# The residual kept in DRAM during two gated networks, block products in the first of them from the seventh pair on, and modulation dots spread over three stages

## The chip, the cores and the metric

The kernel runs on one core of a Trainium2 chip. The number compared is the device time of one execution in microseconds. The engines of the core that matter here are TensorE (PE, with its weight loads on a row of their own, PEld), VectorE (DVE), ScalarE (ACT), GpSimd (POOL) and SyncE (SP). All of them run their instructions in the order in which the program gives them. DMAs are issued from SP, and those that add to what lies at their target are issued from POOL.

## The reference, cut to what matters

One step of a small diffusion backbone on 128 context tokens and 512 latent tokens, width 1024. Two layers: a state-space mixer, a gated convolutional network, a differential attention, and a second gated network. Everything is float32 in and out. In every layer a modulation vector of six parts (shift, scale and gate of both halves) comes from the conditioning:

```python
def modulation(cvec, w, b):
    m = jax.nn.silu(cvec) @ w + b
    return jnp.split(m[:, None, :], 6, axis=-1)

def conv_ffn(h, up_w, conv_w, conv_b, down_w):
    u = dwconv(h @ up_w, conv_w, conv_b)
    a, v = jnp.split(u, 2, axis=-1)
    return (jax.nn.silu(a) * v) @ down_w
...
        xp = xp + p_g1 * op
        xs = xs + s_g1 * os_
        ffn_p = (ffn_up_w[i], ffn_conv_w[i], ffn_conv_b[i], ffn_down_w[i])
        xp = xp + p_g2 * conv_ffn(modulate(xp, norm_ffn_g[i], p_sh2, p_sc2), *ffn_p)
        xs = xs + s_g2 * conv_ffn(modulate(xs, norm_ffn_g[i], s_sh2, s_sc2), *ffn_p)
```

The hidden width of the networks is 2816, that is 22 tiles of 128 rows for `a` and 22 for `v`.

## The kernel before, in words

**Layout.** Activations stand transposed: 8 tiles of 128 features by 640 tokens. Every float32 product is made of three products of rounded operands: each operand is split into a high part (a rounded copy, made by ACT) and a low part (the rest, made by DVE, or by a scaled ACT copy and an accumulating DMA). A weight block of 128x128 against 640 tokens so takes three passes, each in two matmuls of 256 and 384 columns (`HALF`), that is six matmuls.

**Weights.** `weight_units` lists all weight tiles in the order of use. `prefetch` loads them into four raw buffers with DMAs on SP, `cast` makes high and low parts, one or two tiles (`deep`) ahead of their use. For the units in `summed` the low part is made by ACT (a copy times -1) and a DMA from POOL that adds the weight from DRAM; for the others by a DVE subtraction (L107, `wlo`).

**A gated network (`ffn`).** It works in pairs: one tile of `a` and one of `v` (`up`), then the convolution, SiLU and product (`epilogue`, tiles `ca`, `cv`), then a split of the result (`mh`, `ml`). After some pairs (`SUB`) their rows go through the down projection (`project_out`, tile `po`, 8 output tiles), and `gate_add` adds the gated result to the residual `x` on DVE, reading PSUM. The last stretch of the down projection is `project_last`, which also starts the next norm. An ordinary pair is 2 tiles x 8 k-blocks x 6 = 96 matmuls of 320 columns on average. In the second network, pairs 4 to 21 take a seven-product scheme over the whole width (`pair8`, `NS` 4): sums of weight blocks (tiles `s`, made on DVE) and sums of activation blocks (tiles `T`, made once by `operands`), 7 blocks x 4 x 3 = 84 matmuls of 320 columns. In the first network, only pairs 16 to 21 use such a scheme, over half of the width (`pair7`, `NS` 2): 30 k-blocks x 3 = 90 matmuls.

**The dots.** The modulation of the second layer is not a matmul: `mod_rest` loads 48 row tiles `mw` of `modT` (512 KB each) and takes two dot products of each with SiLU of the conditioning (`cbc`), by one DVE instruction of 1024 columns per dot (L620, 96 in all). It is a task that runs between matmuls: `hook` counts ticks, one per k-block (every second block in the product schemes), and a task goes on when its tick has come. All 96 dots lie in the first network.

**Buffers.** The pool `acts` has 19 slots of 640 columns with the tag `f`: 8 of them hold the residual during the networks and the attention, 11 are left for the rest.

**Attention.** For every one of 8 heads: `q`, `k`, `v` tiles, then four blocks of scores (`sl`); the maximum is taken on DVE (`sm`), the exponential on ACT (`e`), the difference of two softmaxes on DVE (`w`), transposes and value products on PE (`wt`, `ov`), and a norm (`rs_v`, `rs_y`, `rs_a`, a small DMA `rsd` and back as `rbc`). `hold` adds a wait to an instruction without data between them; so far it ties scores and value products to earlier instructions. The framework orders each engine's stream from the program and priorities.

## Time and profile before

| | |
|---|---|
| median of three runs | 1849.85 us (1848.75 to 1850.08) |
| profiled execution, own time | 1847.95 us |
| its span | 1846.2 us, mean granted TensorE clock 0.994 |
| PE, PEld busy | 1802.7 us (98%), 1704.8 us (92%) |
| DVE, ACT, POOL busy | 1490.5 us (81%), 1038.7 us (56%), 49.2 us (3%) |
| DMA | 230.28 MB, mean 125 GB/s |
| first network, from its first projection to its last product | 567 to 1026 us |
| attention, heads | 1050 to 1325 us |
| second network | 1391 to 1827 us |

A row of stretches gives, for a window of the span, the busy time and the number of instructions of PE, PEld, DVE, ACT and POOL, then the granted clock, the mean busy share of the 16 DMA engines and their GB/s. PE is counted busy while any matmul is in flight, so that 98% says that there is nearly always one, not that each runs at the full rate; the rate is read from the chain of work, where a piece with its count of matmuls has its length. In the list of groups, the number behind the bar is the busy time, then the mean of one instruction.

### The profile page before, as it was taken

What the parts mean: (1) busy time and instruction counts of PE and PEld (TensorE: products, weight loads), DVE (VectorE), ACT (ScalarE), POOL (GpSimd) and SP (SyncE); (2) the same over time, 40 slices, a digit from 0 to 9 for tenths busy, and PEclk for the clock granted to TensorE, in tenths of its full rate; (3) what the DMA queues carried; (4) which work ended last, traced back from release to release, by engine and by line L of the source; (5) the groups of instructions that cost most, each with busy time, mean ns of one, the idle gap of its engine ahead of it and who ended that gap; (6) DMA issues with size and microseconds to landing.
All of it is one profiled execution on the core that took longest, in us unless ns stands there. A gap on an engine that the chain in (4) does not pass through costs nothing.

```text
span 1846.2 us, 33204 instructions
## 1 busy us (share of the span) xinstructions
PE 1802.7 (98%) x13070; PEld 1704.8 (92%) x13070; DVE 1490.5 (81%) x2969; ACT 1038.7 (56%) x1987; POOL 49.2 (3%) x60
## 2 busy tenths in 40 slices
PE   7999999999999999999999999999999999999997
PEld 5899999999989999999999988888899999999996
DVE  5689999999748999987585878777878877768784
ACT  3489686879326441343353556656636554746561
POOL 0000000000000000000000000000000010101110
PEclk9999999999999999999999999999999999999998
DMA  9844343445533556542122211211124445546451
GB/s 337 264 135 138 99 148 105 121 137 179 187 133 104 194 183 214 194 133 78 57 82 91 80 48 60 65 55 38 55 83 110 104 114 141 126 129 154 122 137 58
DMA packets 90051, 230.28 MB, mean 125 GB/s; under 512 B 10428, under 2 KB 17192, under 8 KB 89768
## 3 DMA queue, kind: packets, MB, share of 16 engines
q1 hardware_dynamic: 81256, 207.13, 34.8%
q0 software_dynamic: 8064, 20.52, 6.6%
q8 instruction: 102, 1.67, 0.4%
q10 hardware_dynamic: 576, 0.52, 0.1%
q14 instruction: 53, 0.43, 0.1%
HBM read 215.29 MB, written 5.96 MB: 120 GB/s over the span
## 4 chain that ended last, share of the span: by engine, by line
PE 86%; DVE 6%; ACT 3%; DMA 3%; issue 2%; SPq 0%; POOL 0%; DVEq 0%; POOLq 0%; ACTq 0%
PE up L110 27%; PE po L110 25%; PE z L110 6%; PE x L110 5%; PE st L110 5%; PE yp L110 3%; PE bc L110 3%; PE q L110 2%; PE k L110 1%; PE modrow L110 1%; PE sl L110 1%; ACT whi L101 1%; PE ov L110 1%; PE v L110 1%; ACT e L101 1%
## 5 line engine op out<-in xcount | busy, mean ns | idle before, releaser
L101 ACT ACTIVATE whi<-raw 128x1024 fp32r<-128x1024 f32 (+3 forms) x243 | 227.8, 939 | 277.3 <-PE po L110 167.4
L107 DVE TENSOR_TENSOR wlo<-raw,whi 128x1024 fp32r<-128x1024 f32 (+3 forms) x207 | 227.0, 1097 | 43.0 <-ACT whi L101 37.5
L104 DVE SCALAR_TENSOR_TENSOR xr<-po,mod,xr 128x256 f32<-128x256 f32 (+2 forms) x279 | 107.8, 432 | 108.9 <-PE po L110 108.8
L110 PE MATMUL po<-mh,whi 128*128 128x256 f32 (+1 forms) x704 | 166.9, 310 | 0.0
L110 PE MATMUL po<-ml,whi 128*128 128x256 f32 (+1 forms) x704 | 166.6, 309 | 0.0
L110 PE MATMUL po<-mh,wlo 128*128 128x256 f32 (+1 forms) x704 | 166.3, 309 | 0.0
L110 PE MATMUL up<-h01l,whi 128*128 128x256 f32 (+1 forms) x596 | 146.2, 308 | 0.0
L110 PE MATMUL up<-h01h,whi 128*128 128x256 f32 (+1 forms) x596 | 146.1, 310 | 0.1
L110 PE MATMUL up<-h01h,wlo 128*128 128x256 f32 (+1 forms) x596 | 145.6, 308 | 0.0
L110 PEld LDWEIGHTS po<-mh,whi 128*128 128x128 f32 x704 | 128.0, 188 | 0.7 <-ACT mh L101 0.5
L110 PEld LDWEIGHTS po<-ml,whi 128*128 128x128 f32 x704 | 128.2, 188 | 0.2 <-DVE ml L107 0.2
L110 PEld LDWEIGHTS po<-mh,wlo 128*128 128x128 f32 x704 | 128.2, 188 | 0.0
L110 PEld LDWEIGHTS up<-h01h,whi 128*128 128x128 f32 x596 | 108.9, 188 | 1.5 <-ACT uraw L101 1.1
L110 PEld LDWEIGHTS up<-h01l,whi 128*128 128x128 f32 x596 | 109.1, 188 | 0.0
L110 PEld LDWEIGHTS up<-h01h,wlo 128*128 128x128 f32 x596 | 109.0, 188 | 0.0
L110 PE MATMUL up<-h11h,whi 128*128 128x320 f32 (+1 forms) x368 | 107.3, 309 | 0.0
L110 PE MATMUL up<-h11l,whi 128*128 128x320 f32 (+1 forms) x368 | 107.2, 309 | 0.0
L110 PE MATMUL up<-h11h,wlo 128*128 128x320 f32 (+1 forms) x368 | 107.1, 309 | 0.0
L104 DVE SCALAR_TENSOR_TENSOR cv<-uraw,fcw,cv 128x511 f32<-128x511 f32 (+1 forms) x176 | 85.3, 545 | 14.8 <-ACT cv L101 14.8
L104 DVE SCALAR_TENSOR_TENSOR ca<-uraw,fcw,ca 128x127 f32<-128x127 f32 (+1 forms) x176 | 86.7, 545 | 8.8 <-ACT ca L101 7.5
L101 ACT ACTIVATE mh<-cv 128x640 fp32r<-128x640 f32 x44 | 32.5, 738 | 88.8 <-DVE cv L107 88.8
L101 ACT ACTIVATE whi<-s 128x512 fp32r<-128x512 f32 (+1 forms) x96 | 52.8, 571 | 52.2 <-DVE s L107 22.7
(531 smaller groups left out, 5074.4 us busy)
## 6 DMA issues: line engine op xcount, KB each, us to landing
raw<-in_w_up SPq DMA_DIRECT2D x88, 512.0 KB, 3.4
mw<-in_modT SPq DMA_DIRECT2D x48, 512.0 KB, 3.8
raw<-in_w_in SPq DMA_DIRECT2D x40, 512.0 KB, 5.5
rb<-rowd SPq DMA_DIRECT2D x40, 512.0 KB, 5.4
raw<-in_w_qkv SPq DMA_DIRECT2D x24, 512.0 KB, 3.3
mr<-in_mod SPq DMA_DIRECT2D x44, 256.0 KB, 5.2
wlo<-in_w_up POOLq DMA_DIRECT2D x17, 512.0 KB, 5.2
mp<-in_modp SPq DMA_DIRECT2D x32, 256.0 KB, 5.4
```

Of the source, the lines that this page charges most:

```text
L101: return self.nc.scalar.activation(out, in_, func, **k)
L104: return self.nc.vector.scalar_tensor_tensor(out, in0, s, in1, op0, op1)
L107: return self.nc.vector.tensor_tensor(out, a, b, op)
L110: return self.nc.tensor.matmul(out, lhsT, rhs, start=start, stop=stop, skip_group_check=more)
```

## The change

Six things are done together.

1. The first network uses `pair8` (`NS` 4) from its seventh pair on (`S0` 6), `pair7` is gone, and both networks project down after 4, 8, 12 and 16 pairs. The units of both networks get their low parts by ACT and DMA (`summed`).
2. In both networks, the residual is not in SBUF while the pairs run. `save` stores its 8 tiles to DRAM (`xd`) before; each of the first four down projections writes its gated result with ACT (`y`), and a DMA from POOL adds `y` to `xd`; `restore` loads the 8 tiles ahead of `project_last`. Attention saves and restores it too.
3. The memory so freed holds the activation sums (`sums`) and, from the first network to the end of attention, the dots' rows (pool `mod`). The `f` slots go from 19 to 11.
4. The dots run in three stages (`DOTS` 3, 34, 48): rows 0 to 2 at the end of the mixer, 3 to 33 in the first network, 34 to 47 in attention. SiLU of the conditioning is computed in the mixer and stored.
5. Each dot gets a wait (`hold`) on the last matmul that stood in the program before it; the number of ticks between dots is set by stage (`gap`, `rest`).
6. The pools follow each other with waits by tile (`reuse_waits`), and attention opens its pool after its first tiles.

```diff
-SUB = ((0, 8), (8, 15), (15, 22)), ((0, 4), (4, 8), (8, 12), (12, 16), (16, 22))
-MIDS = 9, 6
+SUB = (0, 4), (4, 8), (8, 12), (12, 16), (16, 22)
+MIDS = 6
-NS = 2, 4
-S0 = 16, 4
+NS = 4
+S0 = 6, 4
+DOTS = 3, 34, 48
-NF = 19
+NF = 11
...
+    def save(self, i):
+        if not self.xd:
+            self.xd = [self.dram.tile([P, T], F32, tag=f"xd{j}", name=f"xd{j}") for j in range(KT)]
+        self.nc.sync.dma_start(self.xd[i], self.x[i])
+
+    def restore(self):
+        self.open_x()
+        self.x = [self.xslot(f"xr{i}") for i in range(KT)]
+        for i in range(KT):
+            self.nc.sync.dma_start(self.x[i], self.xd[i])
...
-    def project_out(self, h, ks, g, tiles=range(KT)):
+    def project_out(self, h, ks, g, tiles=range(KT), to=None):
...
+            y = to(i)
             for hf in "AB":
-                self.gate_add(i, ps, g, hf)
+                for a, b, c in COND[hf]:
+                    self.act(y[:, a:b], self.cols(ps, hf, a, b), AF.Copy, scale=g[:, i, c:c + 1])
+            self.nc.gpsimd.dma_start(self.xd[i], y, accum_op=ALU.add)
...
-    def mod_rest(self, l, t0, pool):
+    def mod_rest(self, l, t0, t1, cb, alloc, junk_):
...
-                nc.vector.tensor_tensor_reduce(w if c else junk, w, cb[:, c, :], 1.0, 0.0, ALU.mult, ALU.add,
-                                               self.mod[l][:, t, c:c + 1])
-                yield 2 if self.down else 7
+                i = nc.vector.tensor_tensor_reduce(w if c else junk, w, cb[c], 1.0, 0.0, ALU.mult, ALU.add,
+                                                   self.mod[l][:, t, c:c + 1])
+                self.hold(i, [self.last])
+                yield self.gap + c * self.rest
...
         self.start_tiles(h)
         done = 0
-        self.deep = 2 if l else 1
+        self.deep = 2
...
+        self.xctx.close()
+        if not l:
+            self.open_mod()
...
+                    if not l and done == 3:
+                        junk = lambda: self.slot("sq", "junk", BF16, cols=1024, bufs=1)
+                        self.modtask = self.add(self.mod_rest(1, *DOTS[:2], self.cb, self.mod_row, junk), 1)
+                    self.gap, self.rest = 3 if done < S0[0] else 10, 0
...
+                    self.gap = 5 if s else 4
...
+        self.restore()
+        self.project_last(mid, range(*SUB[-1]), self.gate(l, 1), nextnorm, parts="CD" if l else "AB", save=not l)
...
+        self.gap, self.rest = 4, 3
+        early = self.add(self.mod_rest(1, 0, DOTS[0], self.cond_rows(row), row, junk), 8)
+        self.project_last(hy, range(8), self.gate(0, 0), nextnorm, save=True, before=[early])
...
+        self.gap, self.rest = 6, 0
+        dots = self.add(self.mod_rest(1, *DOTS[1:], self.cb, self.mod_row, junk), 10)
```

Line numbers move: what is L104, L107, L110, L620 before is L106, L109, L112, L674 in the changed kernel.

Three places of the order, before and after. First PE in the first network, in the pairs after the eighth (`h01h` and `h01l` are the high and low parts of the activations, `Th` and `Tl` those of their sums). Before, one k-block of an ordinary pair:

```order
L110 MATMUL up<-h01h_6528,whi_9048 128x256
L110 MATMUL up<-h01h_6528,whi_9048 128x384
L110 MATMUL up<-h01l_6529,whi_9048 128x256
L110 MATMUL up<-h01l_6529,whi_9048 128x384
L110 MATMUL up<-h01h_6528,wlo_9049 128x256
L110 MATMUL up<-h01h_6528,wlo_9049 128x384
```

The same engine in a pair of the changed kernel:

```order
L112 MATMUL up<-h01h_6581,whi_8933 128x320
L112 MATMUL up<-h01l_6582,whi_8933 128x320
L112 MATMUL up<-h01h_6581,wlo_8934 128x320
L112 MATMUL up<-Th_7105,whi_8984 128x320
L112 MATMUL up<-Tl_7106,whi_8984 128x320
L112 MATMUL up<-Th_7105,wlo_8985 128x320
```

Blocks of half the tokens against plain and summed operands stand where the six matmuls of a k-block stood: 84 in a pair instead of 96.

Second, DVE in the first network's first down projection before (`xr<-po` is the gated addition to the residual):

```order
L104 SCALAR_TENSOR_TENSOR xr_5172<-po,mod_112,xr_5172 128x128
L107 TENSOR_TENSOR wlo_8298<-raw_8159,whi_8297 128x1024
L620 ISA mw,mod_113<-mw,cbc 128x1024
L620 ISA mod_113 128x1
L620 ISA junk,mod_113<-mw,cbc 128x1024
L620 ISA mod_113 128x1
L620 ISA mw,mod_113<-mw,cbc 128x1024
L620 ISA mod_113 128x1
L104 SCALAR_TENSOR_TENSOR xr_5174<-po,mod_112,xr_5174 128x256 x2
```

In the changed kernel the additions stand on POOL, in the second down projection of the first network, as DMAs from `y` to `xd` between those that make low parts:

```order
L724 DMA ml_8473<-cv 128x640
L357 DMA xd_6145<-y 128x640
L724 DMA ml_8576<-cv 128x640
L357 DMA xd_6146<-y 128x640
L357 DMA xd_6147<-y 128x640
L357 DMA xd_6148<-y 128x640
L357 DMA xd_6149<-y 128x640
L357 DMA xd_6150<-y 128x640
L204 DMA wlo_8954<-in_w_up 128x1024
L357 DMA xd_6151<-y 128x640
L357 DMA xd_6152<-y 128x640
```

The gated addition has left DVE; ACT makes `y`, and eight accumulating DMAs per down projection are new in POOL's queue.

Third, DVE in attention, between the maxima (`sm<-sl`) of the third and the fourth block of a head, before:

```order
L107 TENSOR_TENSOR kl_13327<-k,kh_13326 128x640
L107 TENSOR_TENSOR rs_a<-rs_a,rs_y 128x160
L1305 RECIPROCAL sm<-sm 128x2
L104 SCALAR_TENSOR_TENSOR rs_a<-rs_a 128x160
L107 TENSOR_TENSOR sm<-sm,nlam 128x1
L104 SCALAR_TENSOR_TENSOR rs_y<-rs_a,rs_y 128x160
L104 SCALAR_TENSOR_TENSOR wp<-e_13391,sm,e_13394 128x128
L1297 TENSOR_REDUCE sm<-sl 128x1 x2
L107 TENSOR_TENSOR wlo_13599<-raw_13331,whi_13598 128x1024
```

The same place in a head of the changed kernel:

```order
L109 TENSOR_TENSOR kl_13872<-k,kh_13871 128x640
L109 TENSOR_TENSOR rs_a<-rs_a,rs_y 128x160
L674 ISA mw,mod_116<-mw,cb 128x1024
L674 ISA mod_116 128x1
L106 SCALAR_TENSOR_TENSOR rs_a<-rs_a 128x160
L1317 RECIPROCAL sm<-sm 128x2
L1309 TENSOR_REDUCE sm<-sl 128x1 x2
L106 SCALAR_TENSOR_TENSOR rs_y<-rs_a,rs_y 128x160
L109 TENSOR_TENSOR sm<-sm,nlam 128x1
L109 TENSOR_TENSOR wlo_14150<-raw_13876,whi_14149 128x1024
L1317 RECIPROCAL sm<-sm 128x2
L674 ISA junk,mod_116<-mw,cb 128x1024
```

A dot (`ISA mw,mod<-mw,cb`) stands ahead of the fourth maximum and another behind it; the last steps of the norm and `wp` have moved behind that maximum.

256 lines of the change are left out of this document (123 added, 133 removed).

## The prediction

> **What bounds the kernel now.** First the busy times of the page, then the chain of work that ended last, because only the chain tells the rate of the matmuls (start, length, piece with its count).
>
> ```profile
> PE 1802.7 (98%) x13070; PEld 1704.8 (92%) x13070; DVE 1490.5 (81%) x2969; ACT 1038.7 (56%) x1987; POOL 49.2 (3%) x60
> ```
>
> ```profile
> 582.75 105.61 PE up L110 x720
> 688.36 56.30 PE po L110 x384
> 744.66 98.63 PE up L110 x672
> 843.30 49.80 PE po L110 x336
> 893.10 42.34 PE up L110 x284
> ...
> 962.30 11.64 PE up L110 x78
> 973.94 40.50 PE po L110 x281
> ...
> 1569.40 49.26 PE up L110 x336
> 1618.66 28.16 PE po L110 x192
> ```
>
> Both networks are one unbroken row of matmuls at 147 ns each (105.61/720, 49.26/336). So in them time is the count of matmuls, as long as nobody else is late. Three points of reference: seven ordinary pairs took 98.63 us, 14.09 each; the last six, with the scheme over half of the width, took from 893.10 to 973.94, 80.84 us; four pairs of the second network in the scheme over the whole width took 49.26, 12.32 each. The second network thus already shows the speed that the first is to have.
>
> What the other engines do beside it, by stretches (PE, PEld, DVE, ACT, POOL busy; clock, DMA share, GB/s):
>
> ```profile
> 502.00:562.00 60.00, 60.00 (x466) 53.82 (x466) 29.56 (x65) 19.21 (x32) 0.00 (x0) 1.00 0.41 138
> 582.00:688.00 106.00, 106.00 (x724) 106.00 (x723) 105.59 (x179) 54.52 (x68) 0.00 (x0) 1.00 0.55 182
> 1050.00:1081.00 31.00, 27.71 (x202) 24.94 (x200) 27.05 (x51) 18.62 (x41) 0.00 (x0) 1.00 0.26 85
> 1155.00:1192.00 37.00, 35.48 (x250) 30.81 (x248) 28.74 (x58) 22.63 (x48) 0.00 (x0) 1.00 0.18 58
> 1408.00:1464.00 56.00, 54.21 (x354) 53.95 (x353) 45.16 (x87) 41.49 (x68) 8.00 (x9) 0.97 0.53 108
> 1619.00:1647.00 28.00, 28.00 (x193) 28.00 (x192) 20.42 (x44) 11.16 (x17) 1.75 (x2) 1.00 0.51 144
> 1647.00:1696.00 49.00, 49.00 (x336) 49.00 (x335) 37.54 (x71) 34.13 (x60) 7.88 (x9) 1.00 0.57 127
> ```
>
> The first network has DVE busy for 105.59 of 106 us without a gap on PE. A head of the attention (1155 to 1192) is a different thing: PE is held up for 1.5 us of 37, DVE busy for 28.74.
>
> **The change part by part.** Durations are of the profiled execution, which took 1847.95 us, 1.9 below the median of 1849.85; the sum is made against 1847.95 and 1.9 is added at the end.
>
> *Fewer matmuls.* Pairs 6 to 15 of the first network go from 96 to 84 matmuls, pairs 16 to 21 from 90 to 84: 10x12 + 6x6 = 156 fewer. In time: ten pairs at 14.09 and 80.84 make 221.7 us; sixteen at 12.32 make 197.0. That is -24.7 us, all on the path. The down projections keep their matmuls; five rounds instead of three change nothing in their rate (56.30/384 and 28.16/192 are both 147 ns).
>
> *The gated addition goes from DVE to ACT and a DMA.*
>
> ```profile
> L104 DVE SCALAR_TENSOR_TENSOR xr<-po,mod,xr 128x256 f32<-128x256 f32 (+2 forms) x279 | 107.8, 432 | 108.9 <-PE po L110 108.8
> L101 ACT ACTIVATE uraw<-up 128x320 f32<-128x320 f32 (+2 forms) x111 | 53.9, 491 | 9.4 <-PE up L110 9.1
> L620 DVE CUSTOM_DVE_ANT_0 mw<-mw,cbc 128x1024 f32<-128x1024 f32 x48 | 58.6, 1221 | 0.8
> ```
>
> Three instructions per output tile leave DVE, 1.30 us, and three of ACT from PSUM come, at most 0.49 each by the nearest row (`uraw`). A down projection has eight tiles: ACT gets 11.8 us more in 28 where it has 11.16, DVE 10.4 less. The cover is ACT's idle time, and PSUM, where three tiles stand in turn, each 3.5 us long: 0. Were ACT late, the PSUM banks would come free late and PE would stand.
>
> *The accumulating DMAs.* 64 new ones from POOL, 0.328 MB each. The nearest rows are those of the low parts, which POOL also issues (share of the 16 engines in the stretch):
>
> ```profile
> q0 software_dynamic: 1251, 3.01, 37.4%
> q1 hardware_dynamic: 1296, 3.15, 19.4%
> ...
> wlo<-in_w_up POOLq DMA_DIRECT2D x4, 256.0 KB, 5.9
> ```
>
> In 1647 to 1696, 3.01 MB took 37.4% of 49 us, 18.3 us of all 16 engines: 6.1 us per MB against 3.0 for plain loads (19.4% of 49 us for 3.15 MB). So one `y` costs 2.0 us. A round of four pairs and a down projection lasts 77 us; the engines are busy in it for 0.57x49 + 0.51x28 = 42 us now; eight `y` make 16, and in the first network some twelve dots of the round six rows of 0.524 MB, 9 us. That is 67 of 77 us: room, but loads and low parts queue behind each other in the down projections (14 + 16 + 5 us in 28) and finish later, while a low part has 5.9 us of its own and is used within a pair of 12.3. I take +2 us. The low end is 0; the high end is that an addition into DRAM takes twice as long as one into SBUF, 32 us per round, 83 of 77, four rounds: +24.
>
> The Trainium skill (DMA: Bandwidth & Descriptors, Anatomy of one DMA — SWDGE (gpsimd) path) fits a DMA issued from GpSimd as 2.0 us plus its bytes over 436 GB/s, which would make 0.75 us of moving for a `y`, a term of 0 and a sum 2 us lower; the low parts' 6.1 us per MB above differ from it by more than twice, so the row decides.
>
> *The dots in the first network.* 62 of 96 remain, 75.6 us of DVE at 1.22. The second network's rows are the base (37.54 of 49 in pairs, 20.42 of 28 in down projections): with 7 us of dots in four pairs, 44.5 of 49; with 8 us of dots and without the additions, 18 of 28. The tightest place is pairs 3 and 4, with about ten dots in 28 us, just after the activation sums (1408 to 1464 shows these with DVE at 45.16 of 56 and PE at 54.21). What would be late there is the low part of the next weight. I take +1 us; ends 0 and +6. The SP queue gets the rows (`mw`) past the weight loads as now.
>
> *The dots in attention.* 28 dots, 34.2 us, new to a stage where DVE and PE lean on each other. DVE over one head, with its idle times and what ended them:
>
> ```profile
> 1203.04 0.69 DVE L107 TENSOR_TENSOR wTl<-wt,wTh 128x512 fp32r<-128x512 f32 x1 [1.16 <-ACT wTh L101]
> ...
> 1215.08 0.29 DVE L107 TENSOR_TENSOR vl<-cv,vh 128x128 fp32r<-128x128 f32 x1 [1.16 <-ACT vh L101]
> 1217.15 1.56 DVE L1297 TENSOR_REDUCE sm<-sl 128x1 f32<-128x640 f32 x2 [1.78 <-PE sl L110]
> ...
> 1227.56 1.55 DVE L1297 TENSOR_REDUCE sm<-sl 128x1 f32<-128x640 f32 x2
> 1230.28 1.23 DVE L107 TENSOR_TENSOR wlo<-raw,whi 128x1024 fp32r<-128x1024 f32 x1 [1.17 <-ACT whi L101]
> ```
>
> Four dots fall on a head, 4.9 us, where 37 - 28.74 = 8.3 us are idle. By the order, one stands between the first and second maximum, one ahead of the third (1.16 and 1.78 us idle there), one ahead of the fourth, and one behind it (1.17 idle). Only the one ahead of the fourth stands where DVE has no idle time, from 1217.15 to 1227.56; there 1.2 us come and about 0.7 move behind the maximum: +0.5 us a head, 3.5 for seven heads, and a dot's 1.2 in the first head (27.05 of 31 busy). I take +5 us. Ends: 0, and half of the 34.2, +17.
>
> *The mixer's end.* Six dots and SiLU, some 11 us of DVE, ahead of the drain before the last three tiles. From 502 to 562 DVE is busy for 29.56 of 60: 0; without that cover 3.
>
> *Save and restore.* Eight loads of 320 KB, three times. Their memory comes free with the last block against `T`, two blocks (24 matmuls, 3.5 us) ahead of the end of the last pair; the first addition comes 36 matmuls, 5.3 us, after that. The like load of before landed in 4.6 us:
>
> ```profile
> xr<-in_xT SPq DMA_DIRECT2D x8, 320.0 KB, 4.6
> ```
>
> So 0; if SP stands on them, the next weights are late: +3 at the worst.
>
> Sum: -24.7 + 2 + 1 + 5 = -16.7; 1847.95 - 16.7 + 1.9 = 1833 us.
>
> **The rivals.**
>
> *All of it hidden.* Second network and mixer show DVE with room; then only the matmuls count: 1825 us. Against it: the head's stretch without idle time. 0.13.
>
> *Attention pays half of its dots.* For it: PE already waits in each head; against it: 8.3 us idle per head. +17 instead of +5: 1845 us. 0.15, a quarter of it within 0.2% of now.
>
> *The DMA engines become the bound (slower).* Place: the down projections of the first network. It decides from 3.3 us per `y`: (77 - 42 - 9)/8. Its price at 4.5 us: a round has 42 + 36 + 9 = 87 us of DMA, 10 too much, four rounds, and 1 us in each of four rounds of the second network: 44 instead of 2, so 1875 us. For it: no row shows an addition into DRAM. Against it: low parts are read from DRAM and cost the same per MB as the whole queue. 0.12. The Trainium skill (the same page, Issuing engines are not separate DMA queues) has DMAs of all issuers run on the same 16 engines and interleave; by that rule nothing but the sum of the shares counts, and the trace agrees, with 37.4% and 19.4% side by side.
>
> *The ties hold up DVE (slower).* A dot waits for the last matmul ahead of it in the program, and the additions and low parts behind it on DVE wait too, then PE for them. At 0.4 us for each of 62 dots it is 25 us, 1857 us. Against it: the additions on DVE wait for PE now, 108.8 us of idle time in the row above, and cost PE nothing. 0.05.
>
> **How the numbers follow.** The forecast has 0.55. A measurement can tell about 0.2% from no change. Faster: 0.55 + 0.13 + 0.11 = 0.79; within: 0.04; slower: 0.12 + 0.05 = 0.17. The range reaches from four below the case with all hidden, 1821, to 1852, past the attention's high end with some of the DMA term, and leaves out most of the two slower cases. The forecast's own range is 1826 to 1841.
>
> **What would show it.** Right: a chain with pairs 6 to 21 in pieces of about 12.3 us a pair at 147 ns a matmul, down projections of 28 us; heads of 37 to 38 us; q0's share near 0.55 in the down projections. Wrong: waits of PE for `wlo` or `ml` behind the down projections, `y` DMAs landing after 6 us or more, heads of over 39 us, or DVE idle behind a dot with PE as releaser.

## The result, and the profile after

The changed kernel took 1865.86 us (median of four, 1861.34 to 1867.33), the kernel before beside it 1849.96. The ratio is 1.0078, with a 95% interval of 1.0055 to 1.0101: slower by 0.8%, where 1833 and a gain had been forecast. The profiled execution took 1865.18 us, its span is 1863.4.

Where a stage begins and ends is read from the first and last start of a tile's matmuls: `st` are the first tiles of a stage, `po` the tiles of a down projection. The view of one tile has count, duration in ns (lowest, median, highest), then first and last start. Before, for the first network and the start of attention:

```profile
L110 PE MATMUL st<-h01h,whi x48: 276/332/386, 559.2 to 582.1; 128*128 128x256 f32 x24, 128*128 128x384 f32 x24
L110 PE MATMUL po<-mh,wlo x352: 276/308/343, 688.8 to 1025.4; 128*128 128x256 f32 x165, 128*128 128x384 f32 x11
L110 PE MATMUL st<-h10h,whi x48: 274/334/386, 1025.6 to 1048.7; 128*128 128x256 f32 x24, 128*128 128x384 f32 x24
```

The same rows of the changed kernel:

```profile
L112 PE MATMUL st<-h01h,whi x48: 276/332/386, 559.4 to 582.3; 128*128 128x256 f32 x24, 128*128 128x384 f32 x24
L112 PE MATMUL po<-mh,wlo x352: 274/332/420, 632.7 to 1034.1; 128*128 128x256 f32 x163, 128*128 128x384 f32 x13
L112 PE MATMUL st<-h10h,whi x48: 276/334/582, 1038.1 to 1061.5; 128*128 128x256 f32 x24, 128*128 128x384 f32 x24
```

Read in this way, the stages of one profiled execution each are (us; "gap" is from the last `po` to the first `st` behind it):

| | start of first network | first network | gap | attention | gap | second network |
|---|---|---|---|---|---|---|
| before | 559.2 | 466.2 | 0.2 | 361.2 | 3.3 | 439.3 |
| changed | 559.4 | 474.7 | 4.0 | 366.5 | 1.8 | 440.5 |
| expected by the sum's terms | +0 | 466.2 - 24.7 + 3 | 0 | +5 | 0 | 0 |

Read by these starts, the first network of the kernel before begins at 559.2 us and its second one ends at 1829.4, where the table of the time before has 567 and 1827.

So the loss has one place. The first network has 156 matmuls fewer and should take 441.5 us by their count alone; it took 33.2 more than that. Attention got 5.3 longer, about what had been forecast, and 3.8 came in between. The page's busy line confirms the count, and shows ACT and POOL with the new work:

```profile
PE 1786.0 (96%) x12914; PEld 1687.5 (91%) x12914; DVE 1463.6 (79%) x2907; ACT 1169.8 (63%) x2329; POOL 154.4 (8%) x180
...
q1 hardware_dynamic: 90908, 223.92, 36.9%
q0 software_dynamic: 25344, 62.53, 19.8%
```

What PE waited for from 566 to 1046 us (total us, times, longest), of which the kernel before had nothing in this stage:

```profile
PE up L112 <- DMA wlo<-in_w_up: 18.2, 6, 6.5
PE up L112 <- ACT uraw L103: 3.1, 1, 3.1
PE ms L112 <- ACT sq L103: 2.9, 1, 2.9
PE po L112 <- DMA ml<-cv: 2.4, 3, 1.0
```

The first, second and fourth are 23.7 us of the first network. Most of the rest is the clock, which stood at half in four stretches (us, then PE, PEld, DVE, ACT, POOL busy, clock, DMA share, GB/s):

```profile
684.14:690.97 6.83, 5.94 (x22) 5.94 (x23) 5.46 (x10) 5.68 (x12) 1.76 (x2) 0.50 0.54 136
697.80:701.21 3.41, 3.41 (x15) 3.41 (x14) 2.15 (x5) 0.96 (x2) 0.00 (x0) 0.50 0.41 118
769.48:772.89 3.41, 3.41 (x15) 3.41 (x14) 0.00 (x0) 1.29 (x3) 0.00 (x0) 0.50 0.52 103
933.32:940.14 6.82, 3.36 (x12) 3.37 (x13) 1.67 (x4) 0.29 (x1) 0.00 (x0) 0.50 0.28 94
```

PE was at work in 5.94 + 3.41 + 3.41 + 3.36 = 16.1 us of these, at half the clock, so 8 us were lost; the rest of them lies in the waits and is counted there. 23.7 + 8 is 32 of the 33 us; the last one stays open.

The four full down projections run from 632 to 660, 722 to 751, 807 to 836 and 890 to 919 us. In them the DMA engines have a share of 0.90, 0.87, 0.92 and 0.89. The fullest stretches begin some 10 us into a down projection and end some 10 us behind it (the rows of 735, 815 and 900 us; the other two are mostly pairs):

```profile
735.00:765.00 30.00, 29.24 (x201) 28.98 (x199) 19.54 (x32) 17.44 (x38) 7.02 (x8) 1.00 1.03 266
765.00:815.00 50.00, 45.94 (x302) 45.88 (x303) 41.38 (x79) 33.10 (x57) 8.21 (x10) 0.97 0.67 148
815.00:845.00 30.00, 30.00 (x205) 30.00 (x204) 19.28 (x34) 16.93 (x37) 7.51 (x9) 1.00 1.00 259
900.00:930.00 30.00, 30.00 (x203) 29.85 (x203) 18.71 (x32) 15.77 (x34) 7.62 (x9) 1.00 0.99 257
930.00:994.00 64.00, 56.77 (x375) 56.24 (x373) 47.41 (x87) 44.42 (x73) 9.61 (x11) 0.95 0.69 163
```

In these full stretches PE has hardly a wait, but the share of the DMA engines is 1.0. PE then stands 11 to 15 us behind the end of a down projection, late in the first pair behind it or early in the second (from 764, 847, 851 and 930 us on; behind the first down projection from 675, 682 and 695). The transfers of 632 to 1000 us, with KB each and median us from issue to landing, show what is late:

```profile
raw<-in_w_up SPq DMA_DIRECT2D x34, 512.0 KB, 7.1
mw<-in_modT SPq DMA_DIRECT2D x27, 512.0 KB, 8.0
xd<-y POOLq DMA_DIRECT2D x32, 320.0 KB, 8.6
wlo<-in_w_up POOLq DMA_DIRECT2D x14, 512.0 KB, 7.3
```

In the same stretch of the kernel before, the weights took

```profile
raw<-in_w_up SPq DMA_DIRECT2D x26, 512.0 KB, 4.1
```

The engines show this as waits. DVE stands at a dot in the first down projection and at a weight sum in the fourth, and what is behind these in its row stands with them:

```profile
658.10 1.23 DVE L674 CUSTOM_DVE_ANT_0 junk<-mw,cb 128x1024 bf16<-128x1024 f32 x1 [6.18 <-DMA mw<-in_modT]
...
909.21 0.69 DVE L109 TENSOR_TENSOR s<-raw 128x512 f32<-128x512 f32 x1 [6.57 <-DMA raw<-in_w_up]
```

and PE stands in the first pair behind the fourth, for a low part:

```profile
936.78 0.64 PE L112 MATMUL up<-h01h,wlo 128*128 128x320 f32 x1 [6.46 <-DMA wlo<-in_w_up]
```

This longest wait can be followed back. ACT was done with its copy for the low part at 922.08. POOL issued the DMA at 927.17 only, since a `y` stood ahead of it in POOL's queue and had itself waited, by the profile for a dot:

```profile
924.56 0.88 POOL L357 DMA_DIRECT2D xd<-y  x1 [3.84 <-DVE mod L674]
927.17 0.89 POOL L204 DMA_DIRECT2D wlo<-in_w_up  x1 [1.73 <-DVE wlo L109]
```

It landed 9.6 us after its issue, where 7.3 is the median of its kind. So 5 us went by before POOL issued it, and 2 more than usual until it landed.

The chain of waits ends the stage with such a link as well, where before it had one row of matmuls:

```profile
986.01 8.04 DMA ml<-cv
994.05 0.04 issue
994.10 30.78 PE po L112 x217
```

### The profile page after: what moved, and what is told of

Read it like the earlier page. It is cut to its first block, busy times and chain, and to the rows that moved or that the text cites. A ratio compares the mean times of both kernels' runs of the same rounds, so it can differ in the third digit from the quotient of the medians.

```text
span 1863.4 us, 33793 instructions
## 1 busy us (share of the span) xinstructions
PE 1786.0 (96%) x12914; PEld 1687.5 (91%) x12914; DVE 1463.6 (79%) x2907; ACT 1169.8 (63%) x2329; POOL 154.4 (8%) x180
## 3 DMA queue, kind: packets, MB, share of 16 engines
q1 hardware_dynamic: 90908, 223.92, 36.9%
q0 software_dynamic: 25344, 62.53, 19.8%
## 5 line engine op out<-in xcount | busy, mean ns | idle before, releaser
L103 ACT ACTIVATE whi<-raw 128x1024 fp32r<-128x1024 f32 (+2 forms) x259 | 226.2, 873 | 183.2 <-PE po L112 110.6
L109 DVE TENSOR_TENSOR wlo<-raw,whi 128x1024 fp32r<-128x1024 f32 (+3 forms) x188 | 188.4, 1006 | 41.1 <-ACT whi L103 40.5
L112 PE MATMUL po<-ml,whi 128*128 128x256 f32 (+1 forms) x704 | 165.8, 309 | 2.4 <-DMA ml<-cv 2.4
L112 PE MATMUL po<-mh,whi 128*128 128x256 f32 (+1 forms) x704 | 165.7, 309 | 0.2 <-ACT mh L103 0.2
L112 PE MATMUL po<-mh,wlo 128*128 128x256 f32 (+1 forms) x704 | 165.3, 309 | 0.0
L109 DVE TENSOR_TENSOR wlo<-s,whi 128x512 fp32r<-128x512 f32 x136 | 92.0, 688 | 60.6 <-ACT whi L103 60.2
L112 PE MATMUL up<-h01h,wlo 128*128 128x320 f32 (+2 forms) x400 | 114.6, 316 | 18.2 <-DMA wlo<-in_w_up 18.2
L103 ACT ACTIVATE whi<-s 128x512 fp32r<-128x512 f32 x136 | 84.4, 629 | 74.9 <-DVE s L109 55.9
L112 PE MATMUL up<-Th,whi 128*128 128x320 f32 x408 | 127.9, 313 | 3.1 <-ACT uraw L103 3.1
L112 PEld LDWEIGHTS po<-ml,whi 128*128 128x128 f32 x704 | 127.7, 188 | 3.2 <-DMA ml<-cv 3.2
L112 PEld LDWEIGHTS po<-mh,whi 128*128 128x128 f32 x704 | 127.6, 188 | 0.7 <-ACT mh L103 0.4
L112 PEld LDWEIGHTS po<-mh,wlo 128*128 128x128 f32 x704 | 127.9, 188 | 0.1
L112 PE MATMUL up<-Th,wlo 128*128 128x320 f32 x408 | 127.4, 312 | 0.0
L112 PE MATMUL up<-Tl,whi 128*128 128x320 f32 x408 | 127.3, 312 | 0.0
L106 DVE SCALAR_TENSOR_TENSOR cv<-uraw,fcw,cv 128x511 f32<-128x511 f32 (+1 forms) x176 | 85.7, 547 | 37.5 <-ACT cv L103 37.4
L112 PE MATMUL up<-h01l,whi 128*128 128x320 f32 (+2 forms) x400 | 113.3, 313 | 0.0
L112 PE MATMUL up<-h01h,whi 128*128 128x320 f32 (+2 forms) x400 | 113.3, 313 | 0.0
L112 PE MATMUL up<-h11h,wlo 128*128 128x320 f32 (+1 forms) x368 | 107.3, 309 | 3.0 <-DMA wlo<-in_w_up 3.0
L112 PE MATMUL up<-h11l,whi 128*128 128x320 f32 (+1 forms) x368 | 107.0, 308 | 0.0
L112 PE MATMUL up<-h11h,whi 128*128 128x320 f32 (+1 forms) x368 | 107.0, 308 | 0.0
L106 DVE SCALAR_TENSOR_TENSOR ca<-uraw,fcw,ca 128x511 f32<-128x511 f32 (+1 forms) x176 | 86.8, 547 | 10.0 <-ACT ca L103 8.1
```

What stands on the lines that cost most here:

```text
L103: return self.nc.scalar.activation(out, in_, func, **k)
L106: return self.nc.vector.scalar_tensor_tensor(out, in0, s, in1, op0, op1)
L109: return self.nc.vector.tensor_tensor(out, a, b, op)
L112: self.last = self.nc.tensor.matmul(out, lhsT, rhs, start=start, stop=stop, skip_group_check=more)
```

## The experiments

The theories' letters are the same throughout. A: the DMA engines have too much to do in the first network, and what is late are weights and low parts. B: the rows of the dots alone are too much. C: the place in POOL's queue behind `y` is at fault. D: only the low parts' order is. E: DVE is, by the ties of the dots or by its load. Each verdict is against the kernel before, run beside it; the profile's stage times of all runs stand in a table at the end of this section.

### Parts of the change taken away

```diff
-            self.nc.gpsimd.dma_start(self.xd[i], y, accum_op=ALU.add)
+            if self.wi > len(self.units) // 2:
+                self.nc.gpsimd.dma_start(self.xd[i], y, accum_op=ALU.add)
```

> The changed kernel without the 32 accumulating DMAs of the first network (y is still computed; what the first four down projections give is left out of the residual there). The changed kernel took 1865.9 us; in its first network PE waited 26.6 us and the clock dips behind the waits cost 10.2. Theory A (the DMA engines are full in the down projections, so weights and their low parts come late): the share falls from 1.0 to about 0.5 there, the waits for wlo and the dips go, 1830 us (1825 to 1838). Theory B (the dots' rows mw make the engines full): about half goes, 1848. Theory E (the ties of the dots hold up DVE): 1862 to 1867.

Measured 1845.46 us, ratio 0.998 (0.9967 to 0.9992). The first network took 451.2 us instead of 474.7; the waits for `wlo` went from 18.2 to 3.9, and the weights landed in 3.4 us instead of 7.1. That is A's mechanism, but the time is B's 1848 and not A's 1830: 10 us are left over the matmul count that A had not left. The engines' share over the down projections fell to 0.82, 0.65, 0.61 and 0.65, not to 0.5. In the 30 us from 10 us after the start of the fourth one:

```profile
886.94:916.94 30.00, 30.00 (x208) 30.00 (x207) 19.50 (x34) 16.69 (x35) 1.73 (x2) 1.00 0.65 198
```

```diff
-            if t < t1 - 1:
+            keep = t1 == DOTS[1]
+            if t < t1 - 1 and not (keep and t >= t0):
                 nxt = alloc()
                 nc.sync.dma_start(nxt, a["modT"][t + 1])
...
-nc.vector.tensor_tensor_reduce(w if c else junk, w,
+nc.vector.tensor_tensor_reduce(w if c and not keep else junk, w,
```

> The changed kernel with all dots of the first network in place and at their length, but on one resident row: 30 loads of mw are left out (the modulation of the second layer is wrong). Theory A: a down projection loses about three rows, 5 of its 28 us of DMA, so the share goes from 1.0 to about 0.8 and half of the 37 us goes: 1848 (1840 to 1856). Theory B: all of it goes, 1830. Theory E: nothing changes, 1862 to 1867.

1847.51 us, 0.9979 (0.9959 to 0.9998): the time that A had said, and B's 1830 fell. The first network took 453.3, nearly what it took without `y`, and the waits for `wlo` went to 3.9 here too. But A had said that the share over a down projection goes to 0.8, and it stayed at 0.85 to 0.90. In the same place as above, with `y` there and the rows gone, the engines are as full as in the changed kernel:

```profile
885.23:915.23 30.00, 29.67 (x204) 29.40 (x203) 19.57 (x34) 16.34 (x35) 7.54 (x9) 1.00 1.02 232
```

The other three such stretches have 1.01, 1.02 and 0.95 (in the changed kernel 0.99 to 1.05 in all four). So a full share does not tell what is lost: it cannot show how much is queued behind it. The order in POOL's queue is as it was, so that order alone does not make the loss either. The 62 dots themselves, which stayed, can thus cost no more than a part of the 12 us left over the count; the 21 that went are their rows.

> The changed kernel without the 32 accumulating DMAs of the first network and without 30 of its loads of mw (what the first four down projections give is left out of the residual there, and the dots run on one row). Each alone took away some 22 of the 33 us that the first network takes over 441.5, which is the time before, 466.2, less 24.7. Theory A (together they fill the DMA engines; either one gone makes room): 8 to 10 us more go, 1836 (1832 to 1842). Theory G (each has its own price, and something else holds the last 10 us): 1843 to 1848, as without y alone.

With both edits: 1839.8 us, 0.9952 (0.9937 to 0.9967), first network 447.4, the share in the stretches as above 0.50 to 0.62. Together they give back 27 us where singly they give 23.5 and 21.4: the two are not two prices but one shortage, which either relieves, as A had said (1832 to 1842). G fell.

```diff
-                self.hold(i, [self.last])
+                if t1 != DOTS[1]:
+                    self.hold(i, [self.last])
```

> The changed kernel without the ties of the dots to the matmuls in the first network (those in attention stay). Theories A, B and D: no change, 1862 to 1869. Theory E: the 37 us go for the most part, 1835 to 1850.

1871.83 us, 1.0112 (1.0091 to 1.0134): no gain, rather 6 us worse; PE now waited 11.8 us for `whi` at one place. The ties are not at fault, and E's 1835 to 1850 fell. The rival on them in the prediction is gone. DVE's load, the other half of E, is as before in this run; `dve_lo` below gives DVE more work and is faster.

### Where in POOL's queue, or how much work for the engines

```diff
-            self.nc.gpsimd.dma_start(self.xd[i], y, accum_op=ALU.add)
+            ...
+                self.nc.gpsimd.dma_start(self.xs[i], y)
```

> The changed kernel with the 32 DMAs of y in the first network as plain writes to a scratch tensor (the residual misses these parts). Same queue, same place, same bytes written; nothing is read back and added. Without them the first network took 451 us, with them 475. Theory A: a plain write costs about half of the engines' time, 1.0 us instead of 1.9, and more than half of the 24 us goes, since the engines are then no longer full: 455 to 463 in the first network, 1847 to 1855 in all. Theory C (the place in POOL's queue, ahead of the low parts): 470 to 478, 1862 to 1869.

1849.11 us, 0.9995 (0.9985 to 1.0005), first network 455.3. The place in the queue and the bytes written are the same, and 19 of the 24 us are gone: A's 1847 to 1855, and C's 1862 to 1869 fell. This does not clear the queue altogether. A plain `y` also landed sooner (6.4 us instead of 8.6), so what stands behind it in POOL's queue is held up less, and 5 us of the delay behind the longest wait above came about there. How the loss divides between the queue and the engines is open. The other direction (the scratch tensor is also filled once, by eight plain writes ahead of the network):

```diff
             self.nc.gpsimd.dma_start(self.xd[i], y, accum_op=ALU.add)
+            if self.wi < len(self.units) // 2:
+                self.nc.gpsimd.dma_start(self.xs[i], y, accum_op=ALU.add)
```

> The changed kernel with every accumulating DMA of y in the first network issued twice, the second time to a scratch tensor: 32 more, 1.9 us of the engines each, 15 us in a down projection of 28. Theory A with full engines: each further us of DMA is paid, four rounds, 40 to 60 us more, 1905 to 1926. Theory N (only what is late counts, as the waits behind the down projections show it, and these take the slack of the pairs): 15 to 30 more, 1880 to 1896.

1918.34 us, 1.0374 (1.0346 to 1.0402): 52 us on top of the changed kernel, within A's 40 to 60, and the first network took 527.6. The waits of PE (566 to 1110 us) in it:

```profile
PE up L112 <- DMA wlo<-in_w_up: 45.9, 8, 12.1
PE up L112 <- ACT uraw L103: 15.6, 3, 6.8
```

These four kernels are a series in one quantity, the engines' time for `y`. The share of POOL's queue (packets, MB, share) from 632 to 1000 us, without `y`, with plain writes and as changed:

```profile
q0 software_dynamic: 6896, 17.39, 28.0%
```

```profile
q0 software_dynamic: 9408, 27.76, 34.3%
```

```profile
q0 software_dynamic: 11426, 27.68, 43.0%
```

Times 368 us that is 103, 126 and 158 us: 32 plain writes cost 23 us of all engines, 32 accumulating ones 55. With twice as many, the page's line is

```profile
q0 software_dynamic: 29952, 73.02, 22.5%
```

which is 432 us of 1919.7 against 369 (19.8% of 1863.4), 63 more. Set against the first network:

| engines' time for `y` | first network | of the step, paid |
|---|---|---|
| 0 | 451.2 | |
| 23 us | 455.3 | 4.1 of 23 |
| 55 us | 474.7 | 19.4 of 32 |
| 118 us | 527.6 | 52.9 of 63 |

The share that is paid goes from a sixth over six tenths to more than eight tenths. The first step is no larger than the scatter of a stage between executions, so the four points fit a gradual bend, and they fit as well a threshold somewhere between 23 and 55 us, that is between 0.7 and 1.7 us per `y`. In the changed kernel the engines' mean share from 632 to 1000 us is only 43.0 + 36.2 (SP's queue) = 79%.

### Which link is late

```diff
-        self.summed = (set(up) - set(up[:5]) - set(up[half:half + 5]) - after)
+        self.summed = set(up[half + 5:]) - after
```

> The changed kernel with the low parts of the first network's up weights made by DVE (35 DMAs and 35 ACT copies fewer, 35 DVE subtractions of 0.7 to 1.2 us more). Theory A: the link that came late is gone and the down projections carry some 5 us less of DMA, but weights themselves can still land late: 1840 (1832 to 1850). Theory D (only the order in POOL's queue, low parts behind the y, is at fault): 1830. Theory E (DVE is the place): slower than the changed kernel, 1868 to 1885.

1857.80 us, 1.0045 (1.0029 to 1.006): 8 us better than the changed kernel, between A's 1840 and E's 1868 and outside both ranges; D's 1830 fell. The waits for `wlo` are gone, and the next link has the wait:

```profile
PE po L112 <- DMA ml<-cv: 10.3, 4, 4.0
```

```diff
-            if p < FT - 1:
+            if p + 1 not in [k for _, k in SUB]:
                 self.act(lo, cv, AF.Copy, scale=-1.0)
                 nc.gpsimd.dma_start(lo, cv, accum_op=ALU.add)
```

> The changed kernel with only the four ml of the pairs ahead of a down projection (in both networks) by DVE; the low parts of the up weights stay with ACT and DMA. In the changed kernel PE waited 2.4 us for ml and 18.2 for wlo. Theory A, link by link: 2 to 5 us faster than the changed kernel, 1862 (1858 to 1866), and only both links together give the 20 us. Theory O (ml is the root, and wlo late because of it): 1850 or less.

1862.92 us, 1.0077 (1.0059 to 1.0094), 3 us better than the changed kernel: A, link by link; `ml` is no root of the other. Both edits together:

> As dve_lo (1857.8 us), and the low part of the last pair ahead of each down projection (ml) by DVE instead of ACT and DMA, in both networks: 8 DMAs fewer. In dve_lo PE waited 10.3 us for ml at the start of down projections, with dips of the clock behind it. Theory A: these go, 1848 (1843 to 1853). Theory E: DVE is late itself and the wait gets another name, 1855 to 1862.

1846.25 us, 0.9982 (0.9969 to 0.9994). 20 us better than the changed kernel, where the edits had given 8 and 3 alone, as A had said (1843 to 1853), and 0.2% faster than the kernel before. Rows, dots and all `y` are there; the first network took 450.4 us, and of PE's waits in it no more than these are over 0.7:

```profile
PE up L112 <- ACT uraw L103: 2.6, 1, 2.6
...
PE up L112 <- ACT whi L103: 0.8, 1, 0.8
```

With the kernel's own low parts as the victims of `y` and rows, and DVE with room for them, this is the repair that keeps the change. It shows D half right: the low parts' DMAs are the fragile link. But they add to the load as well, so this run alone does not say by which of the two it works. The stretches from 10 to 40 us after the start of a down projection have a share of 0.96 to 1.03 here too: the engines are as full as in the changed kernel, and what needs them in time is less.

### The rows: how much is their load, how much the wait

```diff
-                nxt = alloc()
-                nc.sync.dma_start(nxt, a["modT"][t + 1])
+                nxt = sink or alloc()
+                i = nc.sync.dma_start(nxt, a["modT"][t + 1])
+                if sink:
+                    self.hold(i, [self.last])
...
-            w = nxt
+            w = w if keep else nxt
```

> The changed kernel with all loads of rows in the first network, each started at the same matmul as its dots, but the dots read one resident row and the loads go to a second one that nobody reads (the modulation of the second layer is wrong). The bytes and the dots stay; what goes is that a dot waits for its row and holds up DVE behind it (13.5 us of DVE in the changed kernel), and that SP waits for dots. Without the loads the first network took 453 us, with them 475. Theory A (the time of the DMA engines is what a row costs): 470 to 478 us for the first network, 1862 to 1869 in all. Theory H (the wait of DVE for late rows is what it costs): 452 to 460, 1844 to 1852.

1859.79 us, 1.0057 (1.0037 to 1.0076): between the theories. By the medians, the loads cost 12 us when nobody waits for them (1859.8 against 1847.5), and the waits of DVE and SP for them 6 more (1865.9); both differences are uncertain by some 4 us. The profiled execution, with a span of 1852.4, was the fastest of its kernel; its 460.1 us for the first network are to be read with that. Mostly A, a third H.

```diff
-                    self.gap, self.rest = 3 if done < S0[0] else 10, 0
+                    self.gap, self.rest = 3 if done < S0[0] else 5, 0
...
-                        self.modtask[1] = self.ticks + 1
+                        self.modtask[1] = self.ticks + 33
```

> The changed kernel with the same rows and dots, but none in the down projections of the first network: all of them between the pairs (gap 5 instead of 10). The bytes of the network stay. Theory A (the down projections alone are too full): 5 of 28 us of DMA leave them, net like the run without rows: 1850 (1842 to 1857). Theory F (a row costs the same wherever it lies): 1862 to 1868. Theory E (DVE's time in the pairs is what counts): 1870 or more, since DVE gets 7 us more in 50 where it has 39.

1873.23 us, 1.0131 (1.0107 to 1.0155): A was wrong here, and the time is what E had said, 1870 or more. The waits of PE say how:

```profile
PE po L112 <- DMA ml<-cv: 12.6, 4, 5.2
PE up L112 <- DMA wlo<-in_w_up: 5.0, 3, 4.1
```

The wait for `wlo` behind the down projections did go down, from 18.2 to 5.0, but one for `ml` ahead of them took its place: a stretch of pairs (first row) now has DVE at 44.18 of 49 us, so the pair's product comes late (its `ml` landed 4.4 us after the issue, in the changed kernel 4.0, so it was issued late), and in the down projection (second row) weights and `y` still fill the engines without any row of dots.

```profile
662.00:711.00 49.00, 48.67 (x327) 47.80 (x327) 44.18 (x82) 32.34 (x59) 7.88 (x9) 1.00 0.76 184
726.00:746.00 20.00, 20.00 (x137) 20.00 (x136) 7.29 (x11) 11.89 (x26) 6.26 (x8) 0.98 1.03 229
```

```diff
-                    self.gap, self.rest = 3 if done < S0[0] else 10, 0
+                    self.gap, self.rest = 3 if done < S0[0] else 1000, 0
...
-                    self.gap = 5 if s else 4
+                    self.gap = 3 if s else 2
```

> The counterpart: from the sixth pair on, all rows and dots of the first network in its down projections (gap 2 and 3 there), none in the pairs. Theory A: two more rows a round, 3 us of DMA, into stretches that are full: 1878 (1870 to 1890). Theory F: 1862 to 1868. Theory E: faster than the changed kernel, 1845 to 1860, since the pairs lose their dots.

1867.40 us, 1.0107 (1.0078 to 1.0137): no change that can be told from the changed kernel, so F's number; A's 1878 and E's 1845 to 1860 fell. The profiled execution took 1876.47, the longest of its kernel. The waits moved again, to `uraw` and `whi` of ACT, while DVE stood at dots whose rows were late:

```profile
PE up L112 <- ACT uraw L103: 13.6, 4, 7.0
PE up L112 <- ACT whi L103: 7.9, 1, 7.9
PE up L112 <- DMA wlo<-in_w_up: 5.5, 4, 2.3
```

```profile
DVE junk L674 <- DMA mw<-in_modT: 24.3, 6, 6.9
```

The last one adds to `rows_pairs`:

```diff
+        for u in after:
+            if u < up[half]:
+                self.summed -= {x for x in up if u <= x <= u + 5}
```

> As rows_pairs, and the low parts of the ten up weights that are made during or just behind a down projection of the first network (of the second network none) by DVE instead of ACT and DMA. Theory A: a round has 5 us less of DMA where it is tight, and the link that was late in the changed kernel is gone: 5 us faster than rows_pairs, 1845 (1838 to 1852). Theory E: slower than rows_pairs by 5 or more.

1868.00 us, 1.0107 (1.0092 to 1.0122), 5 us better than `rows_pairs` as A said, though both are far above A's level (1850 and 1845). 13.7 us of PE's waits were for `ml`, as before.

### How many rows in which stage

`fewer_rows` is `dve_lo_ml` with

```diff
-DOTS = 3, 34, 48
+DOTS = 7, 31, 48
```

and `gap` made to fit (2 and 1 in the mixer, 4, 14, 6 and 7 in the network, 5 in attention). `more_rows` has `DOTS = 3, 38, 48`, gaps of 9 and 4 in the network, and the tie of the next experiment.

> As dve_lo_ml, with 7 rows of dots in the mixer, 24 in the first network and 17 in attention, instead of 3, 31 and 14. Removing all 30 loads took 21 us off the first network, 0.7 each; attention got 5.4 us longer with 28 dots, 0.2 each. Theory A: the first network gets 3 to 5 us shorter, attention 1 to 2 longer, the mixer as before: 2 to 3 us faster than dve_lo_ml, 1845 (1839 to 1850). Theory J (a row costs as much in the mixer or in attention): no faster than dve_lo_ml.

1858.92 us, 1.0051 (1.0035 to 1.0068): 13 us slower than `dve_lo_ml`. The first network was as long as there (449.4), the mixer 9 us longer for four rows, attention 8 for three. J was right, and short of it.

> As ms_after_st, with 35 rows of dots in the first network and 10 in attention, instead of 31 and 14. By the stages a dot cost 0.2 us in attention. Theory A (with the low parts by DVE, the first network has room for rows): attention 1 to 2 us shorter, the first network the same, 1.5 us faster than ms_after_st. Theory M (the first network is at its edge): it pays 0.7 us a row, 3 us, and the sum is 1 to 2 us slower.

1856.17 us, 1.0033 (1.002 to 1.0046): M, but 12 us instead of 2. Four rows more in the first network made it 15 us longer (4 of them came back in the gap behind it), with waits for `ml` (4.9) and for the evacuation by ACT (`po <- ACT y`, 3.9). As far as one execution of each shows, and with the spacing of the dots changed along with their number, the first network and the mixer stand at a bend with 31 and 3 rows, and attention with 14 on the side of more (10 rows gained nothing). A price per row taken from the average of a stage (0.7 us, and 0.2 per dot in attention, as I had it) did not hold for the next row.

### Between the first network and attention

In the changed kernel PE stood 2.9 us at the sums of the norm (`ms`). DVE had been at the norm of the other half when the last gated additions (`xr`) fell due:

```profile
1033.82 0.87 DVE L106 SCALAR_TENSOR_TENSOR nt<-xr,gs,nbc 128x256 f32<-128x256 f32 x2
1035.22 1.28 DVE L106 SCALAR_TENSOR_TENSOR h10l<-nt,mod,h10h 128x256 fp32r<-128x256 f32 x3 [0.54 <-ACT h10h L103]
1036.43 1.39 DVE L106 SCALAR_TENSOR_TENSOR xr<-po,mod,xr 128x256 f32<-128x256 f32 x4
```

```diff
+        self.tie = self.last if half == "B" and self.xd and not self.psb else None
...
+                if tie:
+                    self.hold(m, [tie])
```

> As dve_lo_ml (1846.3 us), and the matmuls of the last norm's sums (ms) ahead of attention are tied to a matmul of attention's first tile, so that PE takes nine matmuls of that tile first, as in the kernel before. In the changed kernel PE stood 2.9 us for the squares there, and 4.0 us lie between the end of the first network and attention, against 0.2 before. Theory K (only the order is at fault): 2 to 3 us go, 1843.5 (1841 to 1846). Theory L (the norm itself is late, since the last down projection has six k-blocks instead of seven to cover it): PE waits behind the nine matmuls instead, 1845 to 1848.

1844.11 us, 0.9972 (0.996 to 0.9984). The order on PE was as wished, but the gap stayed at 3.9 us, and the wait got another name:

```profile
PE st L112 <- DVE xr L106: 3.6, 1, 3.6
```

So K's mechanism fell, although the time lies in its range (1841 to 1846); that is luck. What the first `st` waits for are the last gated additions (`xr`), which DVE reaches only after the norm of the other half. Whether this comes of the six k-blocks of the last down projection, against seven before, was not tried. The 2 us to `dve_lo_ml` are within both kernels' scatter (1841.4 to 1846.3 and 1839.3 to 1850.1), and no stage in the profile accounts for them. Either way this version is faster than both kernels, by 0.3% than the one before and by 1.2% than the changed one.

### All stages

| | first network starts | first network | gap | attention | second network | median |
|---|---|---|---|---|---|---|
| no_y | 561.7 | 451.2 | 4.0 | 366.2 | 441.1 | 1845.5 |
| no_rows | 562.0 | 453.3 | 4.2 | 369.8 | 441.7 | 1847.5 |
| both_off | 559.8 | 447.4 | 4.0 | 366.5 | 443.0 | 1839.8 |
| no_hold | 561.8 | 475.3 | 4.0 | 367.6 | 444.4 | 1871.8 |
| y_plain | 560.4 | 455.3 | 4.2 | 367.7 | 440.1 | 1849.1 |
| y_twice | 562.3 | 527.6 | 4.1 | 364.9 | 442.1 | 1918.3 |
| dve_lo | 561.3 | 461.8 | 4.0 | 367.5 | 442.8 | 1857.8 |
| ml_only | 562.0 | 466.9 | 4.0 | 365.7 | 442.6 | 1862.9 |
| dve_lo_ml | 560.9 | 450.4 | 4.0 | 365.9 | 441.3 | 1846.3 |
| rows_free | 561.4 | 460.1 | 4.0 | 366.2 | 441.4 | 1859.8 |
| rows_pairs | 561.3 | 470.7 | 4.1 | 368.8 | 447.2 | 1873.2 |
| rows_po | 561.9 | 477.7 | 4.0 | 368.6 | 444.6 | 1867.4 |
| rows_pairs_next3 | 562.6 | 473.8 | 4.0 | 366.3 | 440.4 | 1868.0 |
| fewer_rows | 570.3 | 449.4 | 4.2 | 374.3 | 442.6 | 1858.9 |
| ms_after_st | 559.4 | 450.0 | 3.9 | 367.4 | 441.6 | 1844.1 |
| more_rows | 561.4 | 465.5 | 0.2 | 367.1 | 445.0 | 1856.2 |

The stages are of one execution; where code is the same, they scatter: attention with 14 rows from 364.9 to 369.8, the second network from 440 to 447. A difference of a few us between two of them says little by itself.

## Why the prediction was wrong

**The matmuls, -24.7: right as far as it shows.** The count is 156 lower, and where the waits are taken away the first network comes down to 447 to 451 us against 441.5 by count. In `both_off` the four pairs between the second and the third down projection took 49.3 us (746.1 to 795.4), as the 49.26 of the second network had it.

**The accumulating DMAs, +2: this step failed.** Their price was right: 2.0 us each forecast from the low parts' 6.1 us per MB, and 5.9 us per MB on the page after (369 us for 62.53 MB); by the difference of two runs a `y` cost 1.7. The sum over a round was about right as well (67 of 77 us are 87%, measured 79% over the stage). Wrong was what followed from it, "room". The step itself noted 35 us of DMA in the 28 us of a down projection and then took the round's average as the measure; but the pairs, with a share of 0.67 to 0.69 in the rows above, lent too little of their idle engine time. The reason may be that `y` comes in the down projection alone and that weights have four raw buffers; no run has more of these. The traffic finished late, with a share of 1.0 until 10 us behind the down projection, and the low part of the next weight, of which the step knew that it is used within a pair, was late by up to 6.5 us. Instead of 2, the traffic that it summed cost 27 us (`both_off`, 474.7 - 447.4), of which `y` alone gives back 23.5 and the rows alone 21.4. The high end, +24, had been made for a `y` of twice the price. What the runs don't settle is how much of the lateness comes about on the engines and how much in POOL's queue, where low parts stand behind `y`. Of the signs that the prediction had named for itself being wrong, the waits for `wlo` and `ml` came, and `y` landing after 6 us or more (8.6).

**The rival on the DMA engines: right in its mechanism, wrong in its condition.** It was to decide from 3.3 us per `y`, again by the round's average, and got 0.12 for that. At 1.7 to 2.0 us it had already decided: at 1.7 us six tenths of the last step were paid. If there is a point at which it decides, the series puts it between 0.7 and 1.7 us.

**The dots in the first network, +1: right for what it priced, DVE's time.** `no_rows` kept all of it and took the 21 us off. The rows' loads were in the DMA term, and there, by `rows_free`, about a third of their cost was a kind that the sum did not have: DVE standing at a dot whose row is late.

**Attention, +5: the number came, 5.3 (366.5 against 361.2), the way did not.** It was to be half a us in each of seven heads and 1.2 in the first. From the first `q` matmul of a head to that of the next it was 32.3, 37.0, 37.1, 36.8, 36.9 and 36.8 us before, and 32.9, 39.2, 36.9, 37.2, 36.6 and 36.5 in the changed kernel. So one head is 2.2 us longer, 2.8 come behind the last of these starts, and the other heads hardly move. That the sum agrees is luck.

**Mixer, 0: right,** 0.2; by `fewer_rows` four rows more cost 9. **The evacuation by ACT, 0: right** in the changed kernel; `more_rows` shows it as a wait.

**Save and restore, 0:** nothing shows against it. But a term of 3.8 us was missing, the gap between first network and attention. A shorter last down projection or another order of DVE may make it; no run parts the two. In the order of the changed kernel `ms` stands ahead of the first `st`, before behind nine of them; the prediction did not weigh this, and `ms_after_st` shows that it is not the cause.

**The ties, 0.05: right to be small.** Without them it is slower.

The range, 1821 to 1852, left out the measured 1865.9, since both slower rivals had been put outside of it.

## What to carry to other kernels

Sum a shared resource not only over a loop's round but also over the stretch in which its users have to be done. Here 67 of 77 us hid 35 in 28, and stretches of 30 us ran at a share of 1.0. A full stretch is not yet a loss, though: without the rows, or with the low parts on DVE, the stretches stayed full and some 20 us came back. So ask which user has the least slack, and price the change by that user's lateness. Moving the rows about (into pairs, into projections) only renamed the wait here, while giving the tightest user another engine brought back 20 us. And a price per piece from an average does not hold for the next piece once several resources are near full: the first 23 us of `y` were nearly free, the next 32 cost six tenths, and 63 more cost more than eight tenths.

## What the runs showed of the hardware that was not expected

A DMA that adds to its target costs the 16 engines more than twice as much as a plain write of the same bytes from the same queue: 55 us against 23 for 32 transfers of 0.328 MB. The Trainium skill (DMA: Bandwidth & Descriptors, Anatomy of one DMA — SWDGE (gpsimd) path) fits a DMA as 2.0 us plus its bytes over 436 GB/s. By the second part a `y` of this size takes 0.75 us of moving, an estimate; the plain writes agree with 23/32 = 0.72 us, the accumulating ones do not with 1.7. The Trainium skill (the same page, Issuing engines are not separate DMA queues) has DMAs of all issuers run on the same 16 engines. Here this fits: taking away loads that SP issues (`no_rows`) and DMAs that POOL issues (`no_y`) eased the same waits, 18.2 us for `wlo` going to 3.9 in both.

The clock fell at short waits too, but not at all of them. Four waits of PE in the first network had a dip: those of 4.82 and 6.46 us, one of 3.12 (for `uraw`, ending at 685.03) and one of 1.82 (ending at 697.10, the dip beginning at 697.80). Two of 2.25 and 2.06 us (ending at 849.03 and 853.10) had none. The four dips shown above last 3.41 or 6.83 us, and from the first on they begin 4, 25 and 73 steps of 3.41 us later. Laid on this grid, PE was busy for less than half of the step ahead of each dip (1.18, 1.59, 0.41 and 0.40 of 3.41 us), and for half or more of the three steps that hold the two waits without one (2.21, 2.02 and 1.71). The closest two of these:

```profile
694.39:697.80 3.41, 1.59 (x11) 1.33 (x11) 3.41 (x7) 2.05 (x4) 0.00 (x0) 1.00 1.05 186
851.39:854.81 3.42, 1.71 (x11) 1.71 (x12) 3.08 (x7) 0.83 (x2) 0.88 (x1) 1.00 0.57 177
```

That is read off one trace, and no run was made to try it. The Trainium skill (TensorE: Matmul & The Clock Gate, What's actually happening) has the clock halve after an idle window of about 3.4 us. The two long waits agree; the two short ones are below it. So a wait of PE cost here, with its clock, about a third more than its length: 32 us for 23.7 us of waits.
